# A hybrid SSD, attention and feed-forward block: the head norms' transfers on POOL's queue, their multiplications tied behind a weights' split, and two feed-forward items in another place

## The chip, the cores and the metric

The kernel runs on one core of a Trainium2 chip. A core has five engines that run their own instruction queues and wait for one another by semaphores: TensorE (PE, with PEld its weight loads), VectorE (DVE), ScalarE (ACT), GpSimd (POOL) and SyncE (SP, which here only issues transfers). The metric is the device time of one execution in microseconds (us); a kernel's time is the median of its runs. The profile is of one further execution.

## The reference

One layer of a block on x of 512 tokens by 1024 features, in float32:

```python
h = rms_norm(x, norm1_g)
z, xbc, dt_raw, q, k, v, g_ssd, g_attn = split(h @ w_in)
y_ssd  = ssd_branch(z, xbc, dt_raw, ...)     # convolution, chunked state-space scan, gated norm
y_attn = attn_branch(q, k, v, q_norm_g, k_norm_g)
merged = sigmoid(g_ssd) * (y_ssd @ w_ssd_proj) + sigmoid(g_attn) * (y_attn @ w_attn_proj)
x = x + merged @ w_out
u = causal_dwconv(rms_norm(x, norm2_g) @ w_up)          # 3 taps
u_gate, u_val = split(u)
x = x + (silu(u_gate) * u_val) @ w_down
```

In `attn_branch` q, k and v have three groups (dilations 1, 4, 16) of 8 heads of 64 features. Each head's q and k get a norm of their own, the head norm: `q * rsqrt(mean(q*q over the head's 64 features) + eps) * gain`. Then come masked scores, a softmax and the product with v for each group, and the groups are combined by their log sums.

## The kernel before

**Weights.** All products are made in a split form: a weight piece of 128 x 1024 values arrives as `raw` (SP issues the load, `load_piece`, L92), ScalarE casts it to a high part `whi` (L104) and VectorE takes the low part `wlo = raw - whi` (L105). The activations have high and low parts as well (hh, hl), and each piece costs TensorE three products (whi with hh, whi with hl, wlo with hh; `mm_chan`, L144). There are three buffers each of raw, whi and wlo, so pieces are split a little ahead of their use.

**Order of the work.** TensorE's queue runs in the order of the code. In the first part of the kernel (projections, attention, SSD) a scheduler puts the instructions of the other engines in order; from the second norm on VectorE, ScalarE and POOL run in the order of the code too. Side work runs as generators: `start` adds one, and `tick()`, called once or twice for a piece, advances each by one step; a `yield n` makes a generator sit out n ticks. `LAUNCH` (L26) holds after how many ticks the scores of each group begin.

**Head norms.** After the four pieces of one of q and k of one group (`proj_chan`) ScalarE has written the projected rows to `qt` or `kt` and their squares to `qsq`. `norm_heads` (L495 to L519) then goes through these steps: TensorE adds up the squares over each head (`ps_hs`, L499); ScalarE copies the sums to `hs` (L501); four small transfers store them to a DRAM scratch (L503); one loads them back in another shape as `hrv` (L506), so that POOL can raise 128 x 32 values to the power of minus a half (L507); one stores that (L509); two load it spread over all partitions as `hrb` (L513); and VectorE multiplies the four parts of `qt` or `kt` by gain and `hrb` in place (L52, a helper that issues all such three-operand instructions). All eight transfers are issued by SP, in the same queue as the weight loads and as the SSD part's stores (scr_a and scr_e, L369); yields of 2, 4, 1 and 3 ticks stand between the steps. It is done six times (q and k of three groups). `hs`, `hrv` and `hrb` have one buffer each.

**Scores.** `chain` makes the scores of a pair of heads: products of `qt` and `kt` into a PSUM bank (`ps_s`, L537), a mask addition on VectorE that empties the bank (L544), the largest of each row (L550, L554), an exponential on ScalarE, transposes (L568), and the product with v (L579).

**Second norm.** For each block of 128 tokens TensorE transposes the normed rows into two banks (`second_t`, tr_h, L1008), ScalarE casts them to h2h (L1011), VectorE takes the low part (`second_l`, L1016), and ScalarE copies the banks a second time into `act`, as full float32 (`f_copy`, L1037). The next block's transposes need the banks. `add_x1` adds a product to x on VectorE and squares the sum on ScalarE (junk, L984), from which the next block's norm is made.

**Feed-forward.** 22 blocks m of gate and value columns. Some are multiplied plainly (`ps_u`, L1281), some by a Strassen scheme on quarters (L1108) that needs sums of activations s1f to s4f, each split by `split_s` into a high part (ScalarE, sh, L1221) and a low part (VectorE, sl, L1222). The weights of a block are split as uhi (ScalarE, L1086) and ulo (VectorE, L1092) from rawup. `conv_a` and `conv_s` are the taps of the convolution (ScalarE L1144, VectorE L52 on facc), `silu_g` the gate (ScalarE, L1156). `steps` are TensorE's products, with the other engines' work between them in the code's order:

```python
        sum_g(m - 1)
        conv_a(m - 1, 1)
        steps[2]()
        if m in (2, 3):
            split_s(*((2, s3f), (3, s4f))[m - 2])()
        rest(m + 1, "1")
```

Of the kernel before, what the change touches and what calls it, by code (L numbers as in the profile page):

```python
# [8 lines left out]
F32 = mybir.dt.float32  # L9
F32R = mybir.dt.float32r  # L10
AF = mybir.ActivationFunctionType
ALU = mybir.AluOpType
# [10 lines left out]
NEG = -1.0e30  # L23

LAG, PVLAG = 2, 2
LAUNCH = (12, 5, 13)  # L26
COMB = 11
G0, G1, GN = (2, 1, 1, 1), (5, 2, 4, 2), (7, 2, 2)
G2W, YL = 4, 3
# [9 lines left out]
def kernel(  # L39
# [6 lines left out]
    nc = tc.nc  # L46
# [4 lines left out]
    def stt(o, a, s, b, op0, op1):  # L51
        nc.vector.scalar_tensor_tensor(o, a, s, b, op0=op0, op1=op1)  # L52
# [32 lines left out]
    pieces += [chan_piece(w_down, n * 512, 512, k, 2) for n in range(2) for k in range(0, NF, 2)]  # L85
    raws, made = [], []
    used = [0]

    def load_piece():
        n = len(raws)  # L90
# [4 lines left out]
    def make_piece():  # L95
        n = len(made)
        if n == len(pieces):
            return
        if n == len(raws):
            load_piece()  # L100
        raw, shape = raws[n], list(raws[n].shape)
        hi = wp.tile(shape, F32R, tag="whi", name=f"whi{n}", bufs=3)
        lo = wp.tile(shape, F32R, tag="wlo", name=f"wlo{n}", bufs=3)
        nc.scalar.copy(hi, raw)  # L104
        nc.vector.tensor_sub(lo, raw, hi.bitcast(F32))  # L105
        made.append((hi, lo))

    def prefetch(n=2):
# [23 lines left out]
    def start(gen, wait=0):  # L132
        sides.append([gen, wait])
# [41 lines left out]
    qkg = sc[:, 372:374]  # L175
# [67 lines left out]
    warm(4, "a")  # L243
    gain(0)
    gain(1)
    rs1, rest, marks = {}, {}, {}

    def first_norm(t):
        xt = wide(2 * t)
# [244 lines left out]
    def norm_heads(which, g, dest, sq):  # L494
        nm = f"{which}_{g}"  # L495
        scr = scr_q[2 * g + which]
        ps = bank("aux", f"ps_hs{nm}")
        for j in range(4):
            nc.tensor.matmul(ps[j * 32:(j + 1) * 32, :], heads, sq[j], start=True, stop=True)  # L499
        hs = ab.tile([P, S], F32, tag="hs", name=f"hs{nm}", bufs=1)  # L500
        nc.scalar.activation(hs, ps, AF.Identity, bias=epsb, scale=1.0 / 64)  # L501
        for j in range(4):
            nc.sync.dma_start(scr[0, 2 * j:2 * j + 2, :], hs[j * 32:j * 32 + 2, :])  # L503
        yield 2
        rv = ab.tile([P, 32], F32, tag="hrv", name=f"hrv{nm}", bufs=1)
        nc.sync.dma_start(rv, scr[0].rearrange("h (p c) -> (h p) c", c=32))  # L506
        nc.gpsimd.tensor_tensor(rv, rv, nhalf.broadcast_to((P, 32)), op=ALU.pow)  # L507
        yield 4
        nc.sync.dma_start(scr[1].rearrange("h (p c) -> (h p) c", c=32), rv)  # L509
        yield 1  # L510
        rb = ab.tile([P, 4, S], F32, tag="hrb", name=f"hrb{nm}", bufs=1)
        for i in range(2):
            nc.sync.dma_start(rb[i * 64:(i + 1) * 64],  # L513
                              scr[1].rearrange("(j i) t -> i j t", i=2)[i].partition_broadcast(64))
        yield 3
        for j in range(4):
            stt(dest[:, j, :], dest[:, j, :], qkg[:, which:which + 1], rb[:, j, :], ALU.mult, ALU.mult)
            if j == 1:
                yield 1  # L519

    pv = {}
# [140 lines left out]
    for g in range(3):  # L662
        for which in (0, 1):
            proj_chan(g, which)
        if g == 0:
            start(launch(0), LAUNCH[0])
    for g in (1, 2):
        start(launch(g), LAUNCH[g])
    for g in (1, 2):
# [208 lines left out]
    for m2 in range(4):  # L878
        w = next_piece()
        for j in range(2):  # L880
            m = 2 * m2 + j
# [10 lines left out]
    with pool("ysplit") as sp:  # L892
# [14 lines left out]
        for m4 in range(2):  # L907
            pss = [bank("mm", f"ps_sp{m4}_{j}") for j in range(4)]
            for k2 in range(8):
                hi, lo = next_piece()  # L910
# [11 lines left out]
            for j in range(4):  # L922
                m = m4 * 4 + j
# [56 lines left out]
    def add_x1(nh, b, ps):  # L980
        cs = slice(nh * 512, (nh + 1) * 512)
        nc.vector.tensor_add(x1[:, b, cs], x1[:, b, cs], ps)
        junk = n2.tile([P, 512], F32, tag="junk", name=f"junk{nh}_{b}", bufs=2)
        nc.scalar.activation(junk, x1[:, b, cs], AF.Square, accum_out=sums[:, b, nh:nh + 1])  # L984
        if nh == 1:
            nc.sync.dma_start(x1d[b * P:(b + 1) * P, :], x1[:, b, :])
# [16 lines left out]
    def second_t(b, tag="tr"):  # L1003
        for half in range(2):
            ps = bank(tag, f"tr_h{b}_{half}")
            for k in range(4):
                kk = half * 4 + k
                nc.tensor.transpose(ps[:, k * P:(k + 1) * P], hn2[b][:, kk * P:(kk + 1) * P], ident)  # L1008
            tr2[b, half] = p3 = ps.rearrange("p (k t) -> p k t", k=4)
            o = (slice(None), slice(half * 4, half * 4 + 4), slice(b * P, (b + 1) * P))  # L1010
            nc.scalar.copy(h2h[o], p3)  # L1011
# [15 lines left out]
    def quad(kh, th):  # L1027
        return (slice(None), slice(4 * kh, 4 * kh + 4), slice(th * H, (th + 1) * H))
# [4 lines left out]
    f11, f12, f21, f22, s1f, s2f, s3f, s4f = (scratch(i) for i in range(8))  # L1033

    def f_copy(b):
        for half, f in enumerate(((f11, f12), (f21, f22))[b // 2]):
            nc.scalar.copy(f[:, :, b % 2 * P:(b % 2 + 1) * P], tr2[b, half])  # L1037
# [138 lines left out]
    second_scale(1, 0)  # L1176
    ps = ending(2)
    second_t(0)
    add_x1(1, 2, ps)
    second_scale(1, 1)  # L1180
    second_norm(2)
    second_l(0)
    f_copy(0)
    second_scale(2, 0)
    ps = ending(3)
    mp_cm.__exit__(None, None, None)
# [4 lines left out]
    sh = ssp.tile([P, 4, 4, H], F32R, tag="sh", name="sh")  # L1191
    sl = ssp.tile([P, 4, 4, H], F32R, tag="sl", name="sl")
    second_t(1)
    add_x1(1, 3, ps)
    second_scale(2, 1)
    second_l(1)
    f_copy(1)
    second_norm(3)
    up0 = [bank("mm", f"ps_u0_{i}") for i in range(2)]
    wu = [next_piece()]  # L1200
# [19 lines left out]
    def split_s(i, src):  # L1220
        nc.scalar.copy(sh[:, i], src)  # L1221
        return lambda: nc.vector.tensor_sub(sl[:, i], src, sh[:, i].bitcast(F32))  # L1222
# [23 lines left out]
    nc.vector.tensor_sub(s3f, f11, f21)  # L1246
    split_s(0, s1f)()
    nc.gpsimd.tensor_sub(s4f, f12, s2f)
    ops.update({"A11": (h2h[quad(0, 0)], h2l[quad(0, 0)]), "A12": (h2h[quad(1, 0)], h2l[quad(1, 0)]),
                "A22": (h2h[quad(1, 1)], h2l[quad(1, 1)])})  # L1250
    for i in range(4):
# [12 lines left out]
    for m in range(2, NF):  # L1264
        used[0] = first_up + 2 * m + 2
        end = m == NF - 1
        for seq in (raws, made):
            seq += [None] * (used[0] - len(seq))
        if fast(m):
            ba[m] = {k: bank(t, f"ps_u{k}{m}") for k, t in (("a", "mm"), ("b", "mm"), ("c", "aux"), ("d", "tr"))}  # L1270
            steps = [(lambda p=p: product(m, *p)) for p in PRODUCTS]
        else:
            pss = [bank(t, f"ps_u{m}_{i}") for i, t in enumerate(("aux", "tr"))]
            ga[m], ua[m] = pss

            def half(i, part):
                wh, wl = W[m]["w" + "13"[i]]
                seq = [(a, b, k) for a, b in ((wh, h2h), (wh, h2l), (wl, h2h)) for k in range(KD)]
                for n in range(12 * part, 12 * part + 12):
                    a, b, k = seq[n]  # L1280
                    nc.tensor.matmul(pss[i], a[:, k, :], b[:, k, :], start=(n == 0), stop=(n == 23))  # L1281
            steps = [lambda: half(0, 0), lambda: None, lambda: half(0, 1), lambda: None,
                     lambda: half(1, 0), lambda: half(1, 1), lambda: None]
        if fast(m):
            steps[0]()
            conv_a(m - 1, 1)
            rest(m, "3")
            load_up(m + 2)
            steps[1]()
            conv_a(m - 1, 0)  # L1290
            conv_s(m - 1, 1)
            steps[2]()
            cast(m + 1, "1")
# [12 lines left out]
            mul(m - 1)  # L1306
            continue
        steps[0]()
        sum_1(m - 1)
        sum_2(m - 1)  # L1310
        sum_u(m - 1)
        form(m + 1, 3)
        load_up(m + 2)
        if end:
            load_piece()
            load_piece()
            make_piece()
        cast(m + 1, "1")
        sum_g(m - 1)
        conv_a(m - 1, 1)  # L1320
        steps[2]()
        if m in (2, 3):
            split_s(*((2, s3f), (3, s4f))[m - 2])()
        rest(m + 1, "1")
        form(m + 1, 4)
        conv_a(m - 1, 0)
        conv_s(m - 1, 1)
        cast(m + 1, "2")
        steps[4]()
        rest(m + 1, "2")  # L1330
        if end:
            asp[0] = split_act(0, pre, "pre", 2)
            make_piece()
        steps[5]()
        conv_s(m - 1, 0)
        silu_g(m - 1)
        cast(m + 1, "3")
        if not fast(m + 1):
            rest(m + 1, "3")
        cast(m + 1, "b")  # L1340
        if m == 2:
# [81 lines left out]
```

## Time and profile before

| | before |
|---|---|
| median of 3 runs | 1215.61 us |
| lowest and highest run | 1214.03, 1215.69 us |
| the profiled execution | 1215.73 us |
| its span | 1214.0 us, mean TensorE clock 0.996 |
| TensorE busy | 1201.3 us (99%) |
| VectorE busy | 756.7 us (62%) |
| ScalarE busy | 574.4 us (47%) |
| POOL busy | 140.9 us (12%) |
| DMA | 138.95 MB, mean 114 GB/s |

The profile gives the span of the work on the core; the execution's time has a little around it. PEclk is the clock granted to TensorE, 1.0 being full speed: busy time at a lower clock holds less work. In the rows of the timeline stand the start, the duration, the engine, the line, the operation with its output and inputs, how many instructions run together, and in brackets the engine's idle time ahead of it and what ended it.

### The profile page before, as it was taken

What the parts mean: (1) busy time and instruction counts of PE and PEld (TensorE: products, weight loads), DVE (VectorE), ACT (ScalarE), POOL (GpSimd) and SP (SyncE); (2) the same over time, 40 slices, a digit from 0 to 9 for tenths busy, and PEclk for the clock granted to TensorE, in tenths of its full rate; (3) what the DMA queues carried; (4) which work ended last, traced back from release to release, by engine and by line L of the source; (5) the groups of instructions that cost most, each with busy time, mean ns of one, the idle gap of its engine ahead of it and who ended that gap; (6) DMA issues with size and microseconds to landing.
All of it is one profiled execution on the core that took longest, in us unless ns stands there. A gap on an engine that the chain in (4) does not pass through costs nothing.

```text
span 1214.0 us, 15957 instructions
## 1 busy us (share of the span) xinstructions
PE 1201.3 (99%) x6316; PEld 1001.8 (83%) x6316; DVE 756.7 (62%) x999; ACT 574.4 (47%) x890; POOL 140.9 (12%) x95
## 2 busy tenths in 40 slices
PE   9999989999999999999999999999999999999998
PEld 7877767998888888888888888888888999988887
DVE  5214354356789977777744354654779888885542
ACT  4434456367746655465433333433554444444431
POOL 1011111100000201101011000000224242300000
PEclk9999989999999999999999999999999999999999
DMA  5444534422646544424235423344324242425330
GB/s 185 122 106 97 129 97 108 106 72 71 178 126 179 149 121 122 139 71 139 74 81 133 130 88 103 98 143 159 124 76 129 82 114 85 122 87 174 104 121 35
DMA packets 177163, 138.95 MB, mean 114 GB/s; under 512 B 12416, under 2 KB 150256, under 8 KB 176065
## 3 DMA queue, kind: packets, MB, share of 16 engines
q1 hardware_dynamic: 177089, 137.94, 40.2%
q8 instruction: 49, 0.80, 0.3%
q14 instruction: 25, 0.20, 0.1%
HBM read 133.22 MB, written 4.70 MB: 114 GB/s over the span
## 4 chain that ended last, share of the span: by engine, by line
PE 94%; DVE 2%; DMA 1%; ACT 1%; POOL 1%; issue 1%; SPq 0%; DVEq 0%; ACTq 0%; POOLq 0%
PE ps_ssd L144 22%; PE ps_wd L952 10%; PE ps_qk L144 10%; PE ps_u L1281 8%; PE ps_gate L144 7%; PE ps_sp L919 7%; PE ps_v L408 6%; PE ps_wo L952 3%; PE ps_uc L1108 2%; PE ps_ub L1108 2%; PE ps_ua L1108 2%; PE ps_u L144 2%; PE ps_ap L144 2%; PE ps_y L764 1%; PE ps_pv L579 1%; PE ps_s L537 1%
## 5 line engine op out<-in xcount | busy, mean ns | idle before, releaser
L105 DVE TENSOR_TENSOR wlo<-raw,whi 128x1024 fp32r<-128x1024 f32 x154 | 194.6, 1265 | 282.6 <-ACT whi L104 186.9
L104 ACT CAST whi<-raw 128x1024 fp32r<-128x1024 f32 x154 | 161.6, 1050 | 301.9 <-PE ps_ssd L144 62.1
L144 PE MATMUL ps_ssd<-hl,whi 128*128 128x512 f32 x384 | 102.9, 397 | 0.0
L144 PE MATMUL ps_ssd<-hh,whi 128*128 128x512 f32 x384 | 98.4, 398 | 0.0
L144 PE MATMUL ps_ssd<-hh,wlo 128*128 128x512 f32 x384 | 95.4, 390 | 0.0
L952 PE MATMUL ps_wd<-whi,asp 128*128 128x512 f32 x336 | 89.8, 389 | 0.0
L144 PEld LDWEIGHTS ps_ssd<-hh,wlo 128*128 128x128 f32 x384 | 72.1, 188 | 15.9
L144 PEld LDWEIGHTS ps_ssd<-hh,whi 128*128 128x128 f32 x384 | 70.6, 188 | 14.0 <-issue 0.2
L144 PEld LDWEIGHTS ps_ssd<-hl,whi 128*128 128x128 f32 x384 | 70.2, 188 | 14.1 <-issue 0.3
L952 PEld LDWEIGHTS ps_wd<-whi,asp 128*128 128x128 f32 x336 | 63.1, 188 | 13.1
L556 ACT ACTIVATE s<-s,st 128x128 f32<-128x128 f32 (+1 forms) x96 | 39.9, 417 | 37.5 <-DVE st L550 19.7
L952 PE MATMUL ps_wd<-wlo,asp 128*128 128x512 f32 x168 | 51.7, 389 | 0.0
L144 PE MATMUL ps_qk<-hh,whi 128*128 128x512 f32 x192 | 51.1, 409 | 0.0
L1156 ACT ACTIVATE facc<-facc 128x512 f32<-128x512 f32 x22 | 13.9, 633 | 76.1 <-DVE facc L52 76.1
L507 POOL TENSOR_TENSOR hrv<-hrv,nhalf 128x32 f32<-128x32 f32 x6 | 32.5, 5423 | 146.9 <-DMA hrv<-scr_q 146.9
L144 PE MATMUL ps_qk<-hl,whi 128*128 128x512 f32 x192 | 47.7, 390 | 0.0
L144 PE MATMUL ps_qk<-hh,wlo 128*128 128x512 f32 x192 | 47.4, 389 | 0.0
L1092 DVE TENSOR_TENSOR ulo<-rawup,uhi 128x1024 fp32r<-128x1024 f32 x31 | 44.5, 1435 | 4.5 <-ACT uhi L1086 4.5
L144 PEld LDWEIGHTS ps_qk<-hh,whi 128*128 128x128 f32 x192 | 35.9, 194 | 12.7 <-issue 4.5
L1281 PE MATMUL ps_u<-h2h,uhi 128*128 128x512 f32 x176 | 43.7, 390 | 0.0
L1281 PE MATMUL ps_u<-h2l,uhi 128*128 128x512 f32 x176 | 43.5, 389 | 0.0
L1281 PE MATMUL ps_u<-h2h,ulo 128*128 128x512 f32 x176 | 43.5, 389 | 0.0
(317 smaller groups left out, 2491.0 us busy)
## 6 DMA issues: line engine op xcount, KB each, us to landing
raw<-in_w_in_dram SPq DMA_DIRECT2D x100, 512.0 KB
rawup<-in_w_up_dram SPq DMA_DIRECT2D x40, 512.0 KB
raw<-in_w_down_dram SPq DMA_DIRECT2D x22, 512.0 KB
bc<-scr_a SPq DMA_DIRECT2D x8, 1024.0 KB
raw<-in_w_ssd_proj_dram SPq DMA_DIRECT2D x16, 512.0 KB
hrb<-scr_q SPq DMA_DIRECT2D x12, 512.0 KB
eb<-scr_e SPq DMA_DIRECT2D x16, 256.0 KB
raw<-in_w_out_dram SPq DMA_DIRECT2D x8, 512.0 KB
```

Source lines behind the costliest of these rows:

```text
L104: nc.scalar.copy(hi, raw)
L105: nc.vector.tensor_sub(lo, raw, hi.bitcast(F32))
L144: nc.tensor.matmul(ps[:, t0:t0 + nt], a[:, k, c:c + n], b[:, k, t0:t0 + nt], start=(i == 0), stop=(i == total - 1))
L408: nc.tensor.matmul(pss[b], tok(g, kq * 2 + k, b, xx), w[:, k, :], start=(kq == 0 and j == 0 and k == 0), stop=(kq == 3 and j == 2 and k == 1))
L507: nc.gpsimd.tensor_tensor(rv, rv, nhalf.broadcast_to((P, 32)), op=ALU.pow)
L556: nc.scalar.activation(s[:, o:o + nk * P], s[:, o:o + nk * P], AF.Exp, bias=st[:, q, 0, 2 * j + h:2 * j + h + 1], accum_out=st[:, q, 1, 2 ...
L919: nc.tensor.matmul(pss[j], w[:, k, cs], ys[k][xi], start=(k2 == 0 and i == 0 and k == 0), stop=(k2 == 7 and i == 2 and k == 1))
L952: nc.tensor.matmul(pss[b], xs(k0 + k, i)[:, b * P:(b + 1) * P], ww[:, k, :], start=(k0 == 0 and j == 0 and k == 0), stop=(k0 == nk - 2 and ...
L1092: nc.vector.tensor_sub(lo, source(m, x), hi.bitcast(F32))
L1108: nc.tensor.matmul(ba[m][bk][:, c * H:(c + 1) * H], a[:, k, :], b[:, k, :], start=(i == 0), stop=(i == 11))
L1156: nc.scalar.activation(facc[m], facc[m], AF.Silu)
L1281: nc.tensor.matmul(pss[i], a[:, k, :], b[:, k, :], start=(n == 0), stop=(n == 23))
```

## The change

1. `LAUNCH[0]` goes from 12 to 14 ticks: the first group's scores begin later.
2. In `norm_heads` all eight transfers go to POOL's queue. The yields between them go, and one `yield 12` stands ahead of the multiplications. `marks["lo"]` remembers the newest low-part subtraction of the weights, and each pair of multiplications is issued under `tc.issue_after` of it, which tells the scheduler to place them behind that instruction in the queue.
3. `f_copy(0)` and `f_copy(1)` move to right behind `second_t(0)` and `second_t(1)`.
4. `split_s(2, s3f)` moves from the step of m = 2 to right behind `split_s(0, s1f)` and the subtraction that makes s4f, ahead of the loop.

```diff
-LAUNCH = (12, 5, 13)
+LAUNCH = (14, 5, 13)
...
-        nc.vector.tensor_sub(lo, raw, hi.bitcast(F32))
+        marks["lo"] = nc.vector.tensor_sub(lo, raw, hi.bitcast(F32))
...
         for j in range(4):
-            nc.sync.dma_start(scr[0, 2 * j:2 * j + 2, :], hs[j * 32:j * 32 + 2, :])
-        yield 2
+            nc.gpsimd.dma_start(scr[0, 2 * j:2 * j + 2, :], hs[j * 32:j * 32 + 2, :])
         rv = ab.tile([P, 32], F32, tag="hrv", name=f"hrv{nm}", bufs=1)
-        nc.sync.dma_start(rv, scr[0].rearrange("h (p c) -> (h p) c", c=32))
+        nc.gpsimd.dma_start(rv, scr[0].rearrange("h (p c) -> (h p) c", c=32))
         nc.gpsimd.tensor_tensor(rv, rv, nhalf.broadcast_to((P, 32)), op=ALU.pow)
-        yield 4
-        nc.sync.dma_start(scr[1].rearrange("h (p c) -> (h p) c", c=32), rv)
-        yield 1
+        nc.gpsimd.dma_start(scr[1].rearrange("h (p c) -> (h p) c", c=32), rv)
         rb = ab.tile([P, 4, S], F32, tag="hrb", name=f"hrb{nm}", bufs=1)
         for i in range(2):
-            nc.sync.dma_start(rb[i * 64:(i + 1) * 64],
-                              scr[1].rearrange("(j i) t -> i j t", i=2)[i].partition_broadcast(64))
-        yield 3
-        for j in range(4):
-            stt(dest[:, j, :], dest[:, j, :], qkg[:, which:which + 1], rb[:, j, :], ALU.mult, ALU.mult)
-            if j == 1:
+            nc.gpsimd.dma_start(rb[i * 64:(i + 1) * 64],
+                                scr[1].rearrange("(j i) t -> i j t", i=2)[i].partition_broadcast(64))
+        yield 12
+        for i in range(2):
+            with tc.issue_after(marks["lo"].ins):
+                for j in (2 * i, 2 * i + 1):
+                    stt(dest[:, j, :], dest[:, j, :], qkg[:, which:which + 1], rb[:, j, :], ALU.mult, ALU.mult)
+            if i == 0:
                 yield 1
...
     second_t(0)
+    f_copy(0)
     add_x1(1, 2, ps)
     second_scale(1, 1)
     second_norm(2)
     second_l(0)
-    f_copy(0)
...
     split_s(0, s1f)()
     nc.gpsimd.tensor_sub(s4f, f12, s2f)
+    split_s(2, s3f)()
...
-        if m in (2, 3):
-            split_s(*((2, s3f), (3, s4f))[m - 2])()
+        if m == 3:
+            split_s(3, s4f)()
```

Line numbers in the changed kernel are one higher in places (L105 becomes L106). What the instructions' order makes of it, at three places. In the rows, a name's last number counts buffers, and the digits ahead of it say which.

First, SP's queue of before around the norm of q's second group. `hs_1_971` holds its sums, `raw` is a weight load:

```order
L92 DMA raw_1085<-in_w_in_dram 128x8x128
L369 DMA scr_a<-ysb 32x128 x4
L369 DMA scr_e<-ysb 32x128 x4
L503 DMA scr_q<-hs_1_971 2x512 x4
L92 DMA raw_1136<-in_w_in_dram 128x8x128
L92 DMA raw_1214<-in_w_in_dram 128x8x128
L506 DMA hrv_1_1013<-scr_q 128x32
L92 DMA raw_1290<-in_w_in_dram 128x8x128
L509 DMA scr_q<-hrv_1_1013 128x32
L513 DMA hrb_1_1142<-scr_q 64x4x512 x2
```

Now the same norm stands in POOL's queue, behind that of k's first group (`hrv_0_794`):

```order
L508 DMA scr_q<-hrv_0_794 128x32
L511 DMA hrb_0_798<-scr_q 64x4x512 x2
L504 DMA scr_q<-hs_1_971 2x512 x4
L506 DMA hrv_1_977<-scr_q 128x32
L507 TENSOR_TENSOR hrv_1_977<-hrv_1_977,nhalf 128x32
L508 DMA scr_q<-hrv_1_977 128x32
L511 DMA hrb_1_981<-scr_q 64x4x512 x2
```

The norm's transfers no longer share a queue with the weight loads and the SSD stores; on POOL one norm follows the other, and SP keeps the raw, scr_a and scr_e rows alone.

Second, VectorE's queue of before where that norm's multiplications stand (`qt_148` is q of the second group; `s_0_2` and `s_1_0` are mask additions of the first group's scores):

```order
L544 TENSOR_TENSOR s_0_2_1_1116<-ps_s_0_2_1_1106,mneg 128x512
L550 TENSOR_REDUCE st_149<-s_0_2_0_1111 128x2
L550 TENSOR_REDUCE st_149<-s_0_2_1_1116 128x2
L52 SCALAR_TENSOR_TENSOR qt_148<-qt_148,sc,hrb_1_1142 128x512 x2
L105 TENSOR_TENSOR wlo_1217<-raw_1214,whi_1216 128x1024
L52 SCALAR_TENSOR_TENSOR qt_148<-qt_148,sc,hrb_1_1142 128x512 x2
L544 TENSOR_TENSOR s_1_0_0_1187<-ps_s_1_0_0_1181,mneg 128x384
L544 TENSOR_TENSOR s_1_0_1_1193<-ps_s_1_0_1_1182,mneg 128x384
```

And what stands there now:

```order
L544 TENSOR_TENSOR s_0_2_1_1171<-ps_s_0_2_1_1161,mneg 128x512
L550 TENSOR_REDUCE st_149<-s_0_2_0_1166 128x2
L550 TENSOR_REDUCE st_149<-s_0_2_1_1171 128x2
L106 TENSOR_TENSOR wlo_1258<-raw_1255,whi_1257 128x1024
L52 SCALAR_TENSOR_TENSOR qt_148<-qt_148,sc,hrb_1_981 128x512
L544 TENSOR_TENSOR s_1_0_0_1228<-ps_s_1_0_0_1222,mneg 128x384
L544 TENSOR_TENSOR s_1_0_1_1234<-ps_s_1_0_1_1223,mneg 128x384
L554 TENSOR_REDUCE st_149<-s_1_0_0_1228 128x1 x2
L554 TENSOR_REDUCE st_149<-s_1_0_1_1234 128x1 x2
L52 SCALAR_TENSOR_TENSOR qt_148<-qt_148,sc,hrb_1_981 128x512
L106 TENSOR_TENSOR wlo_1331<-raw_1328,whi_1330 128x1024
L52 SCALAR_TENSOR_TENSOR qt_148<-qt_148,sc,hrb_1_981 128x512 x2
```

One multiplication stands ahead of the s_1_0 additions instead of four, behind the split of a later piece. On TensorE the first scores (ps_s_0_0) now follow the products of the fourth piece of the second group's k (ps_qk_1_3) instead of the third (ps_qk_1_2).

Third, ScalarE's queue of before at the start of the feed-forward loop:

```order
L1086 CAST uhi_2_6922<-rawup_1_6851 128x1024
L1221 CAST sh<-act 128x1024
L1086 CAST uhi_3_6948<-rawup_0_6918 128x1024
L1144 ACTIVATE act<-ps_u_1_6854,sc 128x512
L1221 CAST sh<-act 128x1024
L1144 ACTIVATE facc_6967<-ps_u_0_6853,sc 128x512
```

And now:

```order
L1086 CAST uhi_2_6922<-rawup_1_6851 128x1024
L1221 CAST sh<-act 128x1024 x2
L1086 CAST uhi_3_6950<-rawup_0_6918 128x1024
L1144 ACTIVATE act<-ps_u_1_6854,sc 128x512
L1144 ACTIVATE facc_6967<-ps_u_0_6853,sc 128x512
```

The second cast to sh stands ahead of the third block's weights (uhi_3) and of a convolution tap; on VectorE the order at this place stays as it was. In the second norm ScalarE's copies of the first block (L1037) now stand ahead of the square of the third block (junk_2, L984), which before stood ahead of them.

More of the change, by code (lines that the diff above doesn't have):

```diff
@@ L87 @@
     used = [0]
+    marks = {}
     def load_piece():
@@ L245 @@
     gain(1)
-    rs1, rest, marks = {}, {}, {}
+    rs1, rest = {}, {}
     def first_norm(t):
@@ L1193 @@
     second_t(1)
+    f_copy(1)
     add_x1(1, 3, ps)
@@ L1196 @@
     second_l(1)
-    f_copy(1)
     second_norm(3)
```

## The prediction

> **What bounds the kernel now.** I read the page first, then TensorE's waits, then the chain behind each wait in the timeline, then windows to price the waits.
>
> The span and the engines' busy time on the page of before:
>
> ```profile
> span 1214.0 us, 15957 instructions
> PE 1201.3 (99%) x6316; PEld 1001.8 (83%) x6316; DVE 756.7 (62%) x999; ACT 574.4 (47%) x890; POOL 140.9 (12%) x95
> ```
>
> TensorE is busy 99% of the span, and the change leaves its multiplications as they are. So time can come only from its few waits, and from stretches in which it is busy at a lower clock. The waits of TensorE, longest first (what waited, what it waited for, us, times, longest):
>
> ```profile
> PE ps_s L537 <- DVE s L544: 4.6, 1, 4.6
> PE ps_uc L1108 <- DVE facc L52: 2.1, 1, 2.1
> ...
> PE tr_h L1008 <- ACT act L1037: 0.6, 1, 0.6
> ```
>
> The change's parts lie at these three. Each of the first two costs more than its idle time, because the clock afterwards is lower. The windows show it: the stretch around the first wait, then a later stretch of the same kinds of TensorE work without a wait (33 or 34 instructions), and the same pair for the second (86 each).
>
> ```profile
> core 0: us, PE busy (x) PEld busy (x) DVE busy (x) ACT busy (x) POOL busy (x), PEclk, DMA share, GB/s
> 151.09:165.92 14.83, 10.23 (x34) 7.24 (x33) 9.46 (x16) 7.89 (x22) 3.07 (x1) 0.77 0.42 103
> 176.20:182.92 6.72, 6.72 (x33) 5.11 (x32) 5.50 (x8) 0.74 (x2) 0.00 (x0) 1.00 0.31 75
> 899.58:913.00 13.42, 11.34 (x86) 11.16 (x84) 12.18 (x17) 7.17 (x10) 0.73 (x1) 0.87 0.40 111
> 923.90:933.80 9.90, 9.90 (x86) 9.89 (x84) 9.02 (x12) 5.71 (x9) 2.04 (x2) 1.00 0.49 135
> ```
>
> The first wait costs 14.83 − 6.72 = 8.11 us, 1.76 times its 4.60 of idle time; the second costs 13.42 − 9.90 = 3.52 us.
>
> The Trainium skill ("TensorE: Matmul & The Clock Gate", Part 1) lets the clock fall after an idle window of about 3.4 us; the first gap is longer than that, but the second, 2.1 us, was followed by a mean clock of 0.87 as well. By the page's rule only 2.1 us would go with the second wait, and the sum below would end at 1205.7; I go by the row.
>
> **Where the first wait comes from.** In order of time, from the views of SP, VectorE, ScalarE and TensorE (start, duration, what it is, idle time before it and what ended that):
>
> ```profile
> 117.34 0.67 ACT L501 ACTIVATE hs<-ps_hs,epsb 128x512 f32<-128x512 f32 x1
> 124.47 0.75 DVE L52 SCALAR_TENSOR_TENSOR kt<-kt,sc,hrb 128x512 f32<-128x512 f32 x1 [11.78 <-DMA hrb<-scr_q]
> 125.58 1.73 SPq L369 DMA_DIRECT2D scr_a<-ysb  x4
> 129.27 1.12 SPq L503 DMA_DIRECT2D scr_q<-hs  x4
> 151.99 1.42 DVE L52 SCALAR_TENSOR_TENSOR qt<-qt,sc,hrb 128x512 f32<-128x512 f32 x2 [12.35 <-DMA hrb<-scr_q]
> 155.78 1.02 DVE L544 TENSOR_TENSOR s<-ps_s,mneg 128x384 f32<-128x384 f32 x2
> 156.39 2.07 PE L537 MATMUL ps_s<-kt,qt 64*128 64x256 f32 x6 [4.60 <-DVE s L544]
> ```
>
> The sums of q's second group (hs) are ready at 118.0, but their store leaves SP only at 129.27. It stands behind the SSD part's stores (L369), which need a copy that is queued on VectorE behind the multiplication that waited until 124.47. The broadcast row (hrb) lands at 151.99. VectorE has been idle 12.35 us by then, with the mask additions of the next scores queued behind; TensorE needs those for a free bank.
>
> **Part 1: tied multiplications, transfers on POOL, the later start.** The change takes the eight transfers of each norm from SP to POOL and puts each pair of multiplications behind a piece's split. SP no longer holds the norms' store behind the L369 stores, nor those behind the norm. POOL has nothing else to do here. What the eight issues take on SP, and what POOL rows there are:
>
> ```profile
> L503 SPq DMA_DIRECT2D scr_q<-hs x24: 242/256/441, 67.1 to 219.8; - x24
> L513 SPq DMA_DIRECT2D hrb<-scr_q x12: 585/605/675, 83.9 to 231.6; - x12
> L794 POOL TENSOR_TENSOR rv<-rv,nhalf 128x4 f32<-128x4 f32 x8 | 9.5, 1184 | 136.0 <-DMA rv<-scr_v 136.0
> L507 POOL TENSOR_TENSOR hrv<-hrv,nhalf 128x32 f32<-128x32 f32 x6 | 32.5, 5423 | 146.9 <-DMA hrv<-scr_q 146.9
> ```
>
> No row shows a transfer issued by POOL. Its price is bounded by SP's 0.26 us below and POOL's power on 32 columns, 5.42 us, above. I take 1.2, from the nearest short POOL instruction (1184 ns on 4 columns): an issue has little data to touch, and is no cheaper than POOL's own start. A pass by SP, from the first store to VectorE's first multiplication, went so for the first norm and for a late one:
>
> ```profile
> 67.10 1.34 SPq L503 DMA_DIRECT2D scr_q<-hs  x4
> 93.25 0.75 DVE L52 SCALAR_TENSOR_TENSOR qt<-qt,sc,hrb 128x512 f32<-128x512 f32 x1 [5.41 <-DMA hrb<-scr_q]
> 218.87 1.17 SPq L503 DMA_DIRECT2D scr_q<-hs  x4
> 238.51 2.74 DVE L52 SCALAR_TENSOR_TENSOR kt<-kt,sc,hrb 128x512 f32<-128x512 f32 x4 [2.40 <-DMA hrb<-scr_q]
> ```
>
> That is 26.2 and 19.6 us, waits in SP's queue included. I take the longer. With eight issues at 1.2 in place of about 0.3 a pass is 26.2 + 8 × 0.9 = 33.4 us. Now the deadlines, from TensorE's rows: the sums of k's first group, the last piece ahead of the first score, that score, and the first score of the third group:
>
> ```profile
> 91.98 1.07 PE L499 MATMUL ps_hs<-qsq,heads 128*32 128x512 f32 x8
> 122.25 1.98 PE L144 MATMUL ps_qk<-hh,whi 128*128 128x512 f32 x8
> 127.78 0.93 PE L537 MATMUL ps_s<-kt,qt 64*128 64x128 f32 x8
> ...
> 266.42 1.16 PE L537 MATMUL ps_s<-kt,ysb 64*128 64x128 f32 x16
> ```
>
> k's sums are ready at 91.98 + 1.07 + 0.67 = 93.7. The first score now starts one piece later: 127.78 + (127.78 − 122.25) = 133.3. With the pass of 33.4 and 2.1 us for a split and the first multiplications, k is done at 129.2: 4.1 us to spare. q's second group has from 118.0 to about 157 (the four pieces and the scores that now stand ahead of its use): 39 us for 33.4 + 2.2. So TensorE waits for neither, and the whole 8.11 us go. What is late next on VectorE is only its own work, 62% busy. The last norm is the tightest of the later ones: stored at 218.87, it would be done at 218.87 + 33.4 + 2.7 = 255.0, and the third group's first score is at 266.42, 11 us on. The tie itself adds no wait beyond the split, which TensorE needs anyway; if the row isn't there, VectorE holds the next split and the mask additions as before. The end below zero: nothing more than the 8.11 can go here, since TensorE waits nowhere else in this stage. The end above: with a price p for an issue, norms also queue on POOL, whose next pass starts when the last transfer of the one before has been issued, 6.9 us before it is used (231.6 to 238.51 in the rows above). k is then done at 109.8 + 16 p (67 + 16.9 + 8 p until POOL is free, 23.8 + 8 p for the pass, 2.1 for the multiplications). The queue forms above 1.2; TensorE starts to wait at p = 1.5.
>
> **Part 2: the split of the Strassen operand goes ahead.** ScalarE, VectorE and TensorE at the second wait:
>
> ```profile
> 878.44 1.22 DVE L1246 TENSOR_TENSOR act<-act 128x1024 f32<-128x1024 f32 x1
> 879.58 1.22 DVE L1222 TENSOR_TENSOR sl<-act,sh 128x1024 fp32r<-128x1024 f32 x1
> 881.65 1.05 ACT L1086 CAST uhi<-rawup 128x1024 fp32r<-128x1024 f32 x1 [3.44 <-PE ps_u L1281]
> 883.28 1.04 ACT L1221 CAST sh<-act 128x1024 fp32r<-128x1024 f32 x1
> 884.35 2.03 DVE L1222 TENSOR_TENSOR sl<-act,sh 128x1024 fp32r<-128x1024 f32 x1 [3.56 <-ACT sh L1221]
> 901.56 1.53 DVE L52 SCALAR_TENSOR_TENSOR facc<-ps_u,sc,facc 128x511 f32<-128x511 f32 x2
> 903.24 1.19 PE L1108 MATMUL ps_uc<-h2h,uhi 128*128 128x256 f32 x4 [2.08 <-DVE facc L52]
> ```
>
> The cast (883.28) stood behind a weights' cast that waits for TensorE until 881.65, though its source is ready at 879.66 (878.44 + 1.22). Moved ahead, it runs in ScalarE's idle 3.44 us and ends at 880.7; the low part runs from 880.8, in VectorE's idle 3.56 us, and costs nothing there. Everything behind it on VectorE comes up to 3.5 us sooner. The last convolution, ending at 903.1, needs to come 2.1 sooner for TensorE not to wait; so 1.4 us is the margin, and the full 3.52 go. If another wait in this chain holds back over 1.4 of it, part of the 3.52 stays; the ends are −3.52 and 0.
>
> **Part 3: the activations' copies change place.** Here the transposes wait for a bank:
>
> ```profile
> 849.22 0.64 ACT L984 ACTIVATE junk<-x 128x512 f32<-128x512 f32 x1 [0.26 <-DVE x L982]
> 850.24 1.28 DVE L1016 TENSOR_TENSOR h2l<-tr_h,h2h 128x512 fp32r<-128x512 f32 x2
> 850.96 1.18 ACT L1037 COPY act<-tr_h 128x512 f32<-128x512 f32 x2 [1.01 <-DVE h2l L1016]
> 851.60 1.25 PE L1008 MATMUL tr_h<-ident,hn 128*128 128x128 f32 x8 [0.58 <-ACT act L1037]
> ```
>
> The copies no longer wait for the low part, but the norm's square (849.22) now stands behind 1.18 us of copies, and VectorE's low part behind that. So the bank's last reader becomes VectorE: 850.24 + 1.28 + up to 1.18 less what it now need not share with the copies. I put the bank at 0.2 us later than now; ends −0.6 (the wait goes) and +1.2 (all of the copies ahead).
>
> **The sum.** Against the profiled execution, 1215.73 us (span 1214.0, and 1.7 around it; the median of the runs is 1215.61, so no correction): 1215.73 − 8.11 − 3.52 + 0.2 = 1204.3 us.
>
> **The rivals.** (a) Only the feed-forward's wait goes, and the scores wait for something of the same length: 1215.73 − 3.52 = 1212.2. It asks p of about 1.8, by the line above. For it: no row prices POOL's issue. Against: the nearest is 1.2. Chance 0.06.
> (b) Only the head norms' wait goes, since the chain ahead of 901.56 has a second wait: 1207.8. Chance 0.06.
> (c) Neither goes: TensorE's 4.6 us find another cover, and the order on POOL or VectorE does in effect what SP's did: 1215.4 to 1216. Chance 0.05.
> (d) Slower: the issue on POOL costs so much that norms queue there and TensorE waits for k at its first score. It decides from 109.8 + 16 p − 133.3 = 6.6 us of wait, since 6.6 × 1.76 eats the 11.4 gained: p = 1.9. At p = 2.5 the wait is 16.5 us, or 29 with the clock: 1233. At 5.42, the upper bound, it would be about 1315. For it: POOL's power takes 5.42 for 32 columns. Against: the two power rows differ by 4.24 us for 28 columns, so the part without data is about 0.6. Chance 0.09.
> The Trainium skill ("SBUF — State Buffer", the "DVE blocks DMA" trap) speaks for (d): transfers issued by GpSimd starve while VectorE runs operations that take the shared port pair, about 620 ns becoming 3100. It names copy, cast and tensor_scalar for that, and no run here shows it.
>
> **How the numbers follow.** All else, 0.74, is the forecast: 1204.3. Range: down to 1202.8 (part 3 at −0.6, and 0.9 for what windows misprice), up to 1210.0, which holds (b) and a first wait of up to 3.2 us at p = 1.67; that leaves out (a), (c), (d), 0.20. A measurement here can tell 0.2%, 2.4 us, from no change. Faster: 0.74 + 0.06 + 0.06 = 0.86; same: 0.05; slower: 0.09.
>
> **What would show it.** Right: no wait of TensorE for the mask additions (L544) or at the third-quarter products, PEclk 1.0 in both stretches, a pass on POOL of 25 to 35 us, VectorE's waits for hrb gone or short. Wrong: scores waiting for kt, POOL busy or issuing for more than 37 us a norm, the second sl still waiting for its cast.

## The result, and the profile after

The changed kernel takes 1205.35 us (median of 4 runs, 1204.23 to 1205.56) against 1215.31 us (4 runs): a ratio of 0.9918, 95% interval 0.9901 to 0.9935, so 10.0 us less. The profiled executions differ by more, 1215.73 − 1204.23 = 11.5 us; that of before lies just above its four runs, and that of after is the lowest of its own.

The page of after, span and engines:

```profile
span 1202.3 us, 15963 instructions
PE 1196.1 (99%) x6316; PEld 997.8 (83%) x6316; DVE 753.7 (63%) x999; ACT 575.4 (48%) x890; POOL 170.5 (14%) x143
```

TensorE's waits after, as in the list of before:

```profile
PE ps_warma L235 <- DVE ones L156: 1.1, 1, 1.1
PE tr_h L1008 <- DVE h2l L1016: 0.6, 1, 0.6
PE tr_x L219 <- DVE ysb L52: 0.3, 1, 0.3
PE ps_u L145 <- ACT h2h L1011: 0.2, 1, 0.2
```

Both large waits are gone. The wait ahead of the transposes stays as long as it was, but its releaser is VectorE now. The stretches in which the two waits had been, in windows of after:

```profile
core 0: us, PE busy (x) PEld busy (x) DVE busy (x) ACT busy (x) POOL busy (x), PEclk, DMA share, GB/s
142.00:160.00 18.00, 18.00 (x101) 14.09 (x101) 11.38 (x20) 10.99 (x29) 9.97 (x9) 1.00 0.40 95
889.00:903.00 14.00, 14.00 (x103) 13.28 (x103) 12.64 (x18) 7.48 (x11) 2.65 (x2) 1.00 0.47 135
```

TensorE is busy all through, at full clock. Now the head norms of k's first and q's second group on POOL, from the timeline of after:

```profile
94.08 2.10 POOL L504 DMA_DIRECT2D scr_q<-hs  x4 [10.72 <-ACT hs L502]
...
109.63 1.25 POOL L511 DMA_DIRECT2D hrb<-scr_q  x2 [3.20 <-DMA scr_q<-hrv]
117.76 2.11 POOL L504 DMA_DIRECT2D scr_q<-hs  x4 [6.88 <-ACT hs L502]
123.18 0.57 POOL L506 DMA_DIRECT2D hrv<-scr_q  x1 [3.31 <-DMA scr_q<-hs]
126.33 5.44 POOL L507 TENSOR_TENSOR hrv<-hrv,nhalf 128x32 f32<-128x32 f32 x1 [2.59 <-DMA hrv<-scr_q]
132.07 0.62 POOL L508 DMA_DIRECT2D scr_q<-hrv  x1 [0.30 <-POOL hrv L507]
134.48 1.25 POOL L511 DMA_DIRECT2D hrb<-scr_q  x2 [1.79 <-DVE wlo L106]
```

and VectorE's multiplications with SP's SSD stores and the first score:

```profile
116.73 2.10 SPq L370 DMA_DIRECT2D scr_a<-ysb  x4
123.10 1.41 DVE L52 SCALAR_TENSOR_TENSOR kt<-kt,sc,hrb 128x512 f32<-128x512 f32 x2
132.68 0.93 PE L537 MATMUL ps_s<-kt,qt 64*128 64x128 f32 x8
148.26 0.75 DVE L52 SCALAR_TENSOR_TENSOR qt<-qt,sc,hrb 128x512 f32<-128x512 f32 x1
```

The issues of the four stores and of the broadcasts (ns, least, median, most), and the broadcasts' time from issue to landing by the page:

```profile
L504 POOL DMA_DIRECT2D scr_q<-hs x24: 518/530/766, 66.8 to 211.0; - x24
L511 POOL DMA_DIRECT2D hrb<-scr_q x12: 622/630/646, 82.1 to 225.5; - x12
```

```profile
hrb<-scr_q POOLq DMA_DIRECT2D x12, 512.0 KB, 6.7
```

Neither multiplication has a bracket with a wait for hrb: VectorE came to both with hrb there. The SSD stores leave at 116.7 (125.6 before), q's store at 117.8 (129.3 before). An issue takes 0.53 to 0.63 us on POOL, and hrb lands 6.7 us behind its issue in the median, 4.9 to 8.6 in all. The second half of k's hrb was issued at 110.26 and landed 8.4 us later, at 118.7, so k's pass took 24.6 us; that of q's second group took about 26.

The third block's transposes, with the same kind of wait in both, serve as a mark between the parts. They start at 851.60 before and 843.35 after (8.25 us less); from there to the end of the span it is 362.4 and 358.95 us (3.45 less). Of the 8.25, 0.44 lie in the first 18 us (the transposes of x there, tr_x, start at 17.99 before and 17.55 after), where the full clock was granted at 12.2 us before and 9.8 after; the attention stage is left with 7.8.

### The profile page after: what moved, and what is told of

The parts are those of the page before. It is cut to its first block, busy times and chain, and to the rows that moved or that the text cites. A ratio compares the mean times of both kernels' runs of the same rounds, so it can differ in the third digit from the quotient of the medians.

```text
span 1202.3 us, 15963 instructions
## 1 busy us (share of the span) xinstructions
PE 1196.1 (99%) x6316; PEld 997.8 (83%) x6316; DVE 753.7 (63%) x999; ACT 575.4 (48%) x890; POOL 170.5 (14%) x143
## 4 chain that ended last, share of the span: by engine, by line
PE 99%; ACT 0%; DVE 0%; issue 0%; POOL 0%; DVEq 0%
PE ps_ssd L145 22%; PE ps_qk L145 11%; PE ps_u L1282 10%; PE ps_wd L952 10%; PE ps_gate L145 7%; PE ps_sp L919 7%; PE ps_v L409 6%; PE ps_wo L952 3%; PE ps_ua L1108 2%; PE ps_uc L1108 2%; PE ps_ub L1108 2%; PE ps_u L145 2%; PE ps_ap L145 2%; PE ps_s L537 1%; PE ps_y L764 1%; PE ps_pv L579 1%
## 5 line engine op out<-in xcount | busy, mean ns | idle before, releaser
L106 DVE TENSOR_TENSOR wlo<-raw,whi 128x1024 fp32r<-128x1024 f32 x154 | 194.3, 1263 | 315.2 <-ACT whi L105 217.1
L105 ACT CAST whi<-raw 128x1024 fp32r<-128x1024 f32 x154 | 161.7, 1051 | 308.3 <-PE ps_ssd L145 63.1
L778 POOL TENSOR_TENSOR sq<-sq 128x512 f32<-128x512 f32 x8 | 12.4, 1550 | 240.5 <-ACT sq L775 240.5
```

The lines of the kernel that those rows point to most:

```text
L106: marks["lo"] = nc.vector.tensor_sub(lo, raw, hi.bitcast(F32))
L778: nc.gpsimd.tensor_add(sq[:, 0, :], sq[:, 0, :], sq[:, 1, :])
```

## The experiments

Theory: the two waits and the low clock behind them were the whole gain; the first was made by VectorE's multiplications standing too early in its queue, and POOL's queue is one way of shortening the norm's pass. Rivals: it is POOL's queue that counts; it is the later start; the parts depend on one another. Each of the twelve was timed over five rounds beside the kernel before. Its ratio compares the two, and its gain in us is against the median of that kernel there: 1215.09 us for e1 to e4, 1214.40 for e5 to e8, 1214.93 for e9 to e12.

### One part of the change at a time

`e1_split_only` is the kernel before with

```diff
     nc.gpsimd.tensor_sub(s4f, f12, s2f)
+    split_s(2, s3f)()
...
-        if m in (2, 3):
-            split_s(*((2, s3f), (3, s4f))[m - 2])()
+        if m == 3:
+            split_s(3, s4f)()
```

> The kernel before with part 2 alone: the third Strassen operand's split goes ahead of the loop. Theory: the second wait of TensorE (2.1 us) and the half clock behind it both go, so 3.5 us less than before: about 1211.8 against 1215.3, ratio 0.9971; the first wait of 4.6 us stays. By the rule of the Trainium skill (TensorE: Matmul & The Clock Gate, Part 1), under which a gap of 2.1 us does not lower the clock, only 2.1 us would go: 1213.2. Rival: this chain has a second wait and the time stays at 1215.

Measured: 1212.56 us, ratio 0.9979 (0.9966 to 0.9993), 2.5 us less, with an interval that holds both numbers. The wait at ps_uc is gone. From the mark (854.42) to the end of its span of 1213.3 it is 358.9 us, as in the full change. The first wait is there, and longer in this profile than in that of before:

```profile
158.72 2.07 PE L537 MATMUL ps_s<-kt,qt 64*128 64x256 f32 x6 [6.50 <-DVE s L544]
```

`e2_norms_only` is the changed kernel with the split and the copies put back:

```diff
-    split_s(2, s3f)()
...
-        if m == 3:
-            split_s(3, s4f)()
+        if m in (2, 3):
+            split_s(*((2, s3f), (3, s4f))[m - 2])()
```

(and `f_copy` behind `second_l` again, twice).

> Part 1 alone: the changed kernel with the split and the copies put back to where they were before. Theory: the first wait and its half clock go, 7.8 to 8.1 us: about 1207.4 against 1215.3, ratio 0.9935; the second wait of 2.1 us stays. Rival: the two parts depend on one another (a shifted clock window, other loads in flight), and part 1 alone gives under 6 or over 10 us.

Measured: 1208.61 us, 0.9946 (0.9928 to 0.9965), 6.5 us less. The first wait is gone, the second is there, and a new one shows in the SSD stage:

```profile
PE ps_uc L1108 <- DVE facc L52: 2.1, 1, 2.1
PE ps_st L745 <- DVE xdc L739: 1.6, 1, 1.6
```

2.5 and 6.5 add up to 9.0 of the 10.0, and the intervals cover the rest: nothing shows that the parts need one another. The wait at ps_st comes and goes from profile to profile: 0.9 in e6, 0.5 in e10 and e11, 0.2 in e4, none in the change's own or in e9.

`e3_copies_only` is the kernel before with

```diff
     second_t(0)
+    f_copy(0)
...
     second_l(0)
-    f_copy(0)
```

and the same for block 1.

> The kernel before with part 3 alone: the two copies go ahead of the sum and the low part. Theory: the wait of TensorE ahead of the third block's transposes stays at 0.6 us and only its releaser changes from ScalarE's copy to VectorE's low part; time 1215.3 within 0.3. Rival: the wait grows to 1 us or more, since the square and the norm behind it come later: 1216 or more.

Measured: 1215.69 us, 1.0 (0.9984 to 1.0017). The wait is 0.57 us, by VectorE's low part. This kernel also shows what the clock does. Its second wait is as long as that of before:

```profile
904.15 0.71 PE L1108 MATMUL ps_uc<-h2h,uhi 128*128 128x256 f32 x4 [2.03 <-DVE facc L52]
```

but the window around it and the same window around that of e2 (in the second fence; columns as in the windows above) show two different clocks:

```profile
900.49:913.91 13.42, 11.39 (x91) 10.96 (x91) 12.18 (x17) 7.17 (x10) 0.00 (x0) 1.00 0.40 113
```

```profile
893.31:906.73 13.42, 11.31 (x85) 11.14 (x84) 12.18 (x17) 7.16 (x10) 0.50 (x1) 0.87 0.42 114
```

In the same 13.42 us TensorE gets 91 instructions done at the full clock and 85 at 0.87 (86 before). From the mark to the end it is 1213.7 − 852.56 = 361.1 us here, 362.4 before and 359.0 after. So the same gap costs 2.2 us in one execution and 3.5 in another. The Trainium skill ("TensorE: Matmul & The Clock Gate", Part 1) says that the activity window is free-running and that its phase varies from run to run; that agrees with the two outcomes. Its idle window of about 3.4 us as a least gap does not: gaps of 2.1 us lowered the clock in two of these three profiles.

What differs between the three is where the gap lies. In every kept trace the granted clock changes only at a whole number of steps of 3.41 us after it was first granted in full. In before one step, 899.65 to 903.06, holds 1.9 us of the gap; in e2 one step, 893.77 to 897.18, holds all 2.1; and in the step behind either the clock is 0.50. In e3 a step ends at 902.50, inside the gap, which lasts from 902.12 to 904.15: 0.4 us of it fall to one step and 1.65 to the next, and the clock stays at 1.00. Three gaps make a reading and not a rule, and no run moved a gap against the steps on purpose; it fits that the same wait cost 1.3 us more or less by its place alone.

### Which piece of part 1

All of these have parts 2 and 3 of the change. `e4_tie_on_SP` keeps the tie, the tick of the multiplications and the start at 14, and gives the transfers back to SP:

```diff
-            nc.gpsimd.dma_start(scr[0, 2 * j:2 * j + 2, :], hs[j * 32:j * 32 + 2, :])
+            nc.sync.dma_start(scr[0, 2 * j:2 * j + 2, :], hs[j * 32:j * 32 + 2, :])
+        yield 2
...
-        yield 12
+        yield 5
```

(and likewise the other four transfers, with yields of 4 and 1).

> The changed kernel with the norms' eight transfers back on SP's queue, with the yields of before between them (2, 4, 1) and 5 behind them, so that the multiplications come 12 ticks later as in the change; tie, start at 14 and parts 2 and 3 stay. Theory: the wait of before was made by VectorE's early waits for hrb, which held the SSD part's copy and with it SP; with the multiplications late, SP stores q's second group by about 122 and hrb lands by about 145, ahead of its use at 148: no wait, 1205.4 within 1. Rival: POOL's queue is what frees the transfers; on SP the stores still stand behind loads that wait for buffers, VectorE waits 5 us or more for hrb and TensorE for the mask additions: 1208 to 1213.

Measured: 1204.9 us, 0.9915 (0.9897 to 0.9933): the whole gain, without POOL's queue.

`e5_no_tie` is the change without the tie:

```diff
-            with tc.issue_after(marks["lo"].ins):
+            if True:
```

> The changed kernel without the tie: transfers on POOL, the yield of 12 and the later start stay, but VectorE's scheduler may place the multiplications freely; it puts all four of q's second group ahead of the mask additions of the scores s_0_2, right after the scores before. Theory: with a pass of 25 us hrb lands at about 142, VectorE waits about 6 us for it, and the additions come 4 to 5 us later than in the changed kernel; TensorE needs their bank at about 147.6, so it waits 0 to 1 us: 1205 to 1207. Rival: the tie is what removes the wait; without it TensorE waits 4 us or more and 7 us or more come back: over 1212.

Measured: 1212.18 us, 0.9979 (0.9966 to 0.9992), its runs spread from 1208.6 to 1215.1. The rival came true: this is 2.2 us less than before, where part 2 alone gives 2.5, so POOL's queue and the later multiplications gain nothing that can be told without the tie. Its profile is of one of the shorter executions (1209.8 us), and TensorE waits there:

```profile
PE ps_s L537 <- DVE s L544: 1.9, 1, 1.9
PE ps_s L537 <- ACT pt L570: 1.2, 1, 1.2
```

VectorE is held twice by norms that it comes to too early:

```profile
122.67 2.74 DVE L52 SCALAR_TENSOR_TENSOR kt<-kt,sc,hrb 128x512 f32<-128x512 f32 x4 [10.33 <-DMA hrb<-scr_q]
...
145.69 2.74 DVE L52 SCALAR_TENSOR_TENSOR qt<-qt,sc,hrb 128x512 f32<-128x512 f32 x4 [9.46 <-DMA hrb<-scr_q]
```

q's hrb came 3.7 us later than the 142 that I worked with. The 3.1 us of waits, with one stretch of low clock (1.7 us lost), make 4.8 us, and this execution is 4.5 us above the changed kernel's median; why others take up to 5 us more isn't in a trace.

`e6_launch12` has `LAUNCH = (12, 5, 13)`.

> The changed kernel with the first group's scores starting after 12 ticks, as before. Theory: k's first multiplications end at 124.5 and the first score then stands at about 127.2, so nothing waits: 1205.4 within 0.7. Rival: the later start is needed, TensorE waits at the first or the second scores, where the second pair of multiplications now stands behind them: 1207 or more.

Measured: 1204.86 us, 0.9924 (0.9911 to 0.9937): the later start gains nothing that can be told.

`e9_tie_alone`: e4 with `yield 3` in place of `yield 5`, and `LAUNCH` at 12, so that the tie is all that is left of part 1.

> Parts 2 and 3 as in the change; of part 1 the tie alone: the transfers stay on SP with the yields of before (2, 4, 1, 3) and the scores start after 12 ticks. The tie puts k's multiplications behind the copy that the SSD part's stores wait for, and q's first pair behind a split. Theory: VectorE's place of the multiplications is the whole of part 1; SP then stores q's sums at about 121, hrb lands at about 145, and TensorE needs the additions behind it at about 151: no wait, 1204.9 to 1206, the whole gain. Rival: without the two ticks more or without POOL the pass is too long, and TensorE waits 2 us or more: over 1208.

Measured: 1204.12 us, 0.9907 (0.9894 to 0.9921). `e10_late_no_tie`: e4 with the tie taken out.

> As e4 (transfers on SP, yields of 2, 4, 1 and 5, start at 14, parts 2 and 3), but without the tie. VectorE then has k's multiplications ahead of the copy again, and q's first pair ahead of the additions of s_0_2. Theory: SP's stores come late as before, hrb lands at about 150, the additions are needed at 147 to 148: TensorE waits 4 us or more, and 6 us or more of the gain are lost: 1211 to 1216. Rival: the ticks, not the tie, are what counts: 1205 to 1207.

Measured: 1213.47 us, 0.9990 (0.9980 to 1.0001). Part 1's gain is all gone. The tie is all that sets e10 apart from e4; from e9 it differs by the start and two ticks as well. e9 and e10 side by side, first e9: the copy, the SSD stores and q's store on SP, q's multiplications:

```profile
116.33 0.42 DVE L367 COPY ysb<-ps_acsT 128x256 f32<-128x256 f32 x1
116.86 5.20 SPq L370 DMA_DIRECT2D scr_a<-ysb  x4
124.85 1.14 SPq L504 DMA_DIRECT2D scr_q<-hs  x4
145.01 1.41 DVE L52 SCALAR_TENSOR_TENSOR qt<-qt,sc,hrb 128x512 f32<-128x512 f32 x2 [3.00 <-DMA hrb<-scr_q]
```

and e10, with k's first multiplication ahead of the copy and TensorE's wait:

```profile
125.49 0.75 DVE L52 SCALAR_TENSOR_TENSOR kt<-kt,sc,hrb 128x512 f32<-128x512 f32 x1 [12.61 <-DMA hrb<-scr_q]
126.16 0.42 DVE L367 COPY ysb<-ps_acsT 128x256 f32<-128x256 f32 x1
126.61 1.73 SPq L370 DMA_DIRECT2D scr_a<-ysb  x4
130.29 1.12 SPq L504 DMA_DIRECT2D scr_q<-hs  x4
152.45 1.41 DVE L52 SCALAR_TENSOR_TENSOR qt<-qt,sc,hrb 128x512 f32<-128x512 f32 x2 [9.00 <-DMA hrb<-scr_q]
```

```profile
PE ps_s L540 <- DVE s L547: 5.7, 1, 5.7
```

With k's multiplication ahead of it the copy comes 10 us later, q's store 5.4 and q's multiplication 7.4 us later, and TensorE waits. In e4, where only the tie is added to e10, the copy starts at 117.28 and q's store at 126.05, and no score waits for VectorE. The tie moves the multiplications of all six norms; what k's place alone would give wasn't run.

`e12_pool_alone`: the transfers on POOL, with the yields of before, no tie, start at 12.

> Parts 2 and 3 as in the change; of part 1 POOL's queue alone: yields of before (2, 4, 1, 3), no tie, start at 12. VectorE has all four of q's multiplications ahead of a split and of the additions of s_1_0. Theory: the transfers on POOL no longer stand behind the SSD part's stores, hrb lands at 143 to 146, the additions end at about 151, just when TensorE needs them: a wait of 0 to 1.5 us and large differences between runs: 1205 to 1209. Rival: without the tie nothing is gained, and the 4 to 5 us of wait stay: over 1211.

Measured: 1210.74 us, 0.9961 (0.9948 to 0.9973), 4.2 us less than before where part 2 alone gives 2.5. So POOL's queue without the tie gains 1 to 2 us of the attention stage's 8; the expectation's range just missed it. The first wait is gone, but VectorE is still held by hrb (20.5, 18.9 and 9.0 us in all for rows of k, of q, and of the norm whose row is named ysb), and TensorE waits further on:

```profile
PE ps_pt L571 <- ACT s L559: 1.4, 1, 1.4
PE ps_s L540 <- ACT pt L573: 1.3, 1, 1.3
```

These and a low clock behind one of them make some 4 us of the 6.6 that it is longer than e9; the rest isn't placed.

### What a slow pass on POOL would have cost

`e7_pow3` and `e8_pow4` lengthen each pass:

```diff
         nc.gpsimd.tensor_tensor(rv, rv, nhalf.broadcast_to((P, 32)), op=ALU.pow)
+        for _ in range(2):
+            nc.gpsimd.tensor_tensor(rv, rv, ones[:, 0:1].broadcast_to((P, 32)), op=ALU.pow)
```

(3 in e8).

> The changed kernel with two more powers (to the first power, which keeps the values) of 128 x 32 on POOL in each norm, about 11 us more for each pass: as if each of the eight issues took 1.9 us in place of 0.56. By the deadlines: k's hrb lands at about 129 where 131 is needed, no wait; POOL is then free for q's second group at 122 in place of 117.8, its hrb lands at about 158 where VectorE needs it at about 154: TensorE waits about 3.5 us, with the half clock 6 us: about 1211. Rival: the norms have no deadline near, and the time stays at 1205.4; or POOL's added work slows VectorE or the transfers elsewhere and it is 1215 or more.

> The changed kernel with three more such powers in each norm, about 16.5 us more for each pass. By the deadlines: POOL's passes queue (34 us each where a norm comes every 25), k's hrb lands at about 140 and TensorE's first score waits about 8.6 us, then q's and k's second groups some 11 and 7 us: 27 us of idle time, with the half clock behind it 27 to 47 us: 1232 to 1252, slower than before. Rival: the norms have no deadline near: under 1215.

Measured: 1217.68 us, 1.0028 (1.0016 to 1.0039), and 1247.49 us, 1.0276 (1.0263 to 1.0290). Waits in e7:

```profile
PE ps_s L539 <- DVE s L546: 8.2, 1, 8.2
...
PE ps_s L539 <- DVE kt L52: 0.9, 1, 0.9
```

The deadlines are there, but e7's waits are 9.1 us where I expected 3.5, and its time is past the 1215 that I named for POOL's work slowing the other engines. VectorE isn't slowed: it is busy for 753.6 us here and 753.7 in after. POOL's rows say what is:

```profile
125.19 1.25 POOL L513 DMA_DIRECT2D hrb<-scr_q  x2 [1.72 <-DMA scr_q<-hrv]
126.43 2.11 POOL L504 DMA_DIRECT2D scr_q<-hs  x4
133.94 0.57 POOL L506 DMA_DIRECT2D hrv<-scr_q  x1 [5.40 <-DMA scr_q<-hs]
```

Where a norm's stores follow the broadcast of the one before at once, POOL waits 5.4 us for them, 6.6 for k's, against 3.3 and 1.9 for the same norms in the change. My model let the passes follow one another without that. TensorE's longest in e8:

```profile
PE ps_s L539 <- DVE kt L52: 10.9, 1, 10.9
PE ps_s L539 <- DVE s L546: 10.3, 1, 10.3
PE ps_pt L570 <- ACT s L558: 5.4, 2, 4.8
PE ps_s L539 <- ACT pt L572: 1.7, 2, 0.9
```

In e8 the waits of TensorE at scores and transposes add up to 28 us for the 27 expected.

### A version that may be better

`e11_early_low` is e4 with the start at 12, and

```diff
     second_scale(1, 1)
+    second_l(0)
     second_norm(2)
-    second_l(0)
     second_scale(2, 0)
```

> A version that may be better than both kernels: e4 with the start at 12, and in the second norm the first block's low part ahead of the third block's norm. Theory: the low part frees the transposes' bank 0.6 us or more earlier, TensorE's wait of 0.6 us there goes, and the norm behind it has time: 1204.3 against 1204.9 for e4, 0.6 us that the times can hardly show but the waits can. Rival: the norm is then late and TensorE waits at a later transpose by as much or more.

Measured: 1204.67 us, 0.9910 (0.9897 to 0.9924). The wait at the transposes is gone, and others have come in its place (the first stood in after too, once and 0.2 us long):

```profile
PE ps_u L145 <- ACT h2h L1014: 0.5, 2, 0.2
PE ps_u L145 <- DVE h2l L1019: 0.2, 1, 0.2
```

So 0.6 us went and 0.5 came back. e4, e6, e9 and e11 can't be told from the changed kernel by their intervals. The least of them, e9, is the tie with parts 2 and 3; since part 3 alone changes nothing (e3), the tie with part 2 should do, but that pair wasn't run.

## Why the prediction was right, and where not

- **The sum.** 1204.3 was predicted; the profiled execution took 1204.23, the median of the runs 1205.35. Against the two profiles the terms hold: 7.8 for 8.11, 3.45 for 3.52, 0 for the 0.2 of part 3. That the sum comes within 0.1 us of the profiled execution is partly luck, since that was the lowest of after's four runs and the profile of before lay above its runs. Over many runs the parts give less than the sum has, 6.5 for part 1 (e2), 2.5 for part 2 (e1) and 10.0 for the whole change where the sum has 11.4. What a wait costs differs between executions of the same work: the second cost 3.5 us in the profile that was priced and 2.2 in e3's, while the first lasted 4.6 (before), 5.8 (e3) and 6.5 us (e1), so that here the profile had the shortest. I took one execution's price as the price. The range's lower end has a slip of 0.2: from 1204.3, which holds +0.2 for part 3, to part 3 at −0.6 it is 0.8, so 1202.6 and not 1202.8.
- **Part 1, the mechanism.** Right that VectorE's early multiplication holds the copy, the copy SP's stores, those the norm's, and that TensorE then lacks the additions: the rows of e9 and e10 show it link by link, and e4 against e10 shows that the tie sets it off. Wrong in the piece that does it. The prediction gave the gain to POOL ("SP no longer holds the norms' store") and priced the tie at nothing ("adds no wait beyond the split"). The tie alone gives the whole gain of this part (e9), POOL without the tie 1 to 2 us (e12) or nothing (e5), and SP serves as well as POOL (e4). The later start, from which I worked a deadline, isn't needed (e6).
- **Part 1, the price.** An issue on POOL was put at 1.2 us; it takes 0.53 to 0.63. A pass was put at 33.4; k's takes 24.6. Both erred to the safe side, and k is done at 124.5 where 129.2 was worked out and 132.7 needed.
- **The slower rival.** Slower passes do turn the gain into a loss: at two powers more, as if p were 1.9, the time is 2.8 parts in a thousand above before. The prediction had put the point of no gain at p = 1.9, and that the two agree is luck: it had TensorE wait 6.6 us for k at its first score, where e7 shows 0.9 there and 8.2 at the mask additions behind q's second group, and it left out that stores behind a broadcast land late. Its p was also over three times the real price. Of the stall of transfers issued by GpSimd that the Trainium skill ("SBUF — State Buffer", the "DVE blocks DMA" trap) describes, nothing is seen in after, where issues on POOL take 0.52 to 0.77 us; but no run here sets a copy or cast of VectorE beside them on purpose, so its rule isn't tried.
- **Part 2.** Right, by e1's waits and by the mark. Its size is 2.2 to 3.5 us, by where the gap lies against the clock's steps, and neither my reading (always the half clock behind) nor that of the Trainium skill (never after 2.1 us) is the rule.
- **Part 3.** Right that nothing would be won; the bank's last reader is VectorE's low part, as worked out, and the wait stayed at 0.57.

## What to carry to other kernels

An instruction that waits in an in-order queue costs what stands behind it, and that can be a copy which another queue's transfers need: look for the wait's first cause a whole pass earlier, and move the waiting instruction behind the work that doesn't need it before moving its transfers. When a change has several pieces, price each by what would remain if it alone were made; here one line gave, as far as the times can tell, the whole of the largest part. A wait's price read from one execution is one draw: compare the same stretch in a second profile before adding it to a sum.

## What the runs showed of the hardware

- After a gap TensorE's clock falls to half for whole multiples of 3.41 us, and the fall can begin while the gap lasts (by the clock's events in the traces): not at all at the 2.0 us of e3; once 3.41 at the 1.9 of e5 and the 2.1 of before and e2; twice at 4.6 to 6.5 (before, e1, e3, e10); three times at e7's 8.2; four times at e8's 10.9 and 10.3. Waits close together count together: in e12 two of 1.4 and 1.3 us with 1.9 us of work between had one, and in e8 one of 4.8 and one of 0.8 with 2.4 us of work between had three. Each 3.41 us that TensorE works through at the half clock loses 1.7 us, as in the window of before: 13.42 × (1 − 0.87) = 1.7.
- An issue of a transfer holds POOL for 0.53 us (each of the four small stores), 0.57 (a load of 128 x 32) and 0.63 (a broadcast to 64 x 4 x 512) in after, where SP takes 0.26, 0.38 and 0.61 in before.
- Small stores that follow a large broadcast on POOL's queue within 1.2 us are waited for 5.2 to 7.0 us (e7, e8), at 1.4 to 1.5 us behind it 3.8 to 3.9 (e5, e12), and with 6 us or more between 1.6 to 3.3 (after).
